# A decoder layer on one core: VectorE takes the products of the sample tokens' attention, and its loads go to GpSimd's queue

## The chip, the core and the metric

The kernel runs on one core of one Trainium2 chip. The metric is the device time of one execution in microseconds. The kernel before takes 1683.91 us, the median of three runs (1677.45 to 1688.59). A profiled execution of it took 1681.99 us, of which the profile's span, from the first to the last instruction, is 1680.2 us.

## What is computed

One layer of a hybrid decoder, for 1024 prompt tokens and 32 sample tokens (8 sequences of 4 tokens, with caches). From the normalised input a projection gives a convolution branch, queries, keys and values of 12 heads, and two gates. The heads stand in three groups of four with window and dilation (128, 1), (512, 4), (2048, 16). What matters here is the attention of the sample tokens, whose keys and values come mostly from the caches:

```python
def _dilated_sample(q, k_all, v_all, slopes, window, dil, L):
    ...
    j = jnp.arange(window // dil + 1)
    idx = L + jnp.arange(T)[:, None] - j[None, :] * dil
    kg = k_all[:, jnp.maximum(idx, 0)]
    vg = v_all[:, jnp.maximum(idx, 0)]
    s = jnp.einsum('bthd,btjhd->bhtj', q, kg) * (1.0 / math.sqrt(Dh))
    s = jnp.where(idx >= 0, s - slopes * j * dil, NEG_INF)
    p = softmax(s)
    o = jnp.einsum('bhtj,btjhd->bthd', p, vg)
```

The outputs of the three groups are combined by their softmax denominators, projected, gated, mixed with the convolution branch and added to the input; a SwiGLU feed-forward layer, a gated per-layer embedding and a final norm follow. (The lines above are cut and shortened.)

## The kernel before

All products of the prompt and of the projections run on TensorE. The float32 operands are split into a high and a low part, and each product takes three matmuls (lines 120 to 122: high by high, high by low, low by high). All 1056 tokens are handled in three chunks of 352 columns. Weights come in slabs of 512 KB (`wst`, issued from SP's queue, line 93); ScalarE makes the high part (`whi`, line 103) and VectorE the low part (`wlo`, line 104).

The stages in order: the norm of the input and the embedding's projection; the projections for the convolution and the gates, with the depthwise convolution on VectorE; then, from about 336 us, the attention; the convolution's output projection (VectorE multiplies each result by its gate, `et`, line 891, 24 times, 8 tiles by 3 chunks; the gates come from `gcd`, line 886); the attention's output projection (line 956 on VectorE, line 957 on GpSimd); and then the output projection, the feed-forward layer and the tail.

The attention runs over two pairs of heads, and in each over the three groups. For each group q, k and v are projected, TensorE makes the scores of the prompt (`ps_s`, line 824, into two banks), and VectorE empties these banks with bias and row maximum (`S` and `mcol`, line 829). After the third group the prompt's softmax follows: transposes on TensorE (line 747), copies out of PSUM on ScalarE or, for pair 0, every second one on VectorE (`pt`, line 753), and the product with the values (`N`, line 724).

The attention of the sample tokens runs beside all this, without TensorE. `sample_ops(pair, g)` makes it for one pair and group. The 128 partitions hold 64 rows (32 tokens by 2 heads) twice, the halves taking 64 cached positions each. `load` fetches the bias (`sbias`, line 552) and the queries (`sq`, line 555), the latter from a scratch tensor in DRAM (`scr`, line 862) that is written after the group's projections. `steps` then goes over the 64 positions in eight tiles of 8 positions by 64 elements (`kt`, a ring of four buffers, two loads of 64 partitions each, line 584), and `new` adds a ninth tile with the new tokens' keys or values (lines 592, 595, 598). For keys, `k_part` multiplies a tile by the query on GpSimd (line 558) and sums over the elements on VectorE (line 559). `smax` makes the softmax (lines 563 to 566). For values, `v_part` multiplies by the weights on GpSimd (line 571 for the first tile, line 573 for the others) and adds up on VectorE (line 574); line 606 sums the rest. After the third group `sample_out` joins the groups (lines 610 to 636) into the 32 sample columns of `ohi` and `olo`, which the attention's output projection reads.

These steps wait in a list and are handed out between the projections, some at a time. The order in which each engine runs its instructions is then fixed before the program starts, by a scheduler that places each instruction by its priority and by its own estimates of durations. On the chip each engine's queue runs in that order, and an instruction that waits holds up all that stand behind it on the same queue. SP's queue issues nearly all loads and stores, ScalarE's the copies of the caches, GpSimd's none.

Of the kernel before, what the change touches and what calls it, by code (L numbers as in the profile page):

```python
# [13 lines left out]
OP = mybir.AluOpType  # L14
# [18 lines left out]
SOFF = (0, 132, 261, 390)  # L33
# [14 lines left out]
def hybrid_layer(ctx: ExitStack, tc: tile.TileContext, I, O):  # L48
    nc = tc.nc
    te, ve, ac, gp, sy = nc.tensor, nc.vector, nc.scalar, nc.gpsimd, nc.sync  # L50
# [253 lines left out]
    scr = [[dram.tile([3, 32, 128], F32, name=f"scr{i}{g}") for g in range(3)] for i in range(2)]  # L304
# [224 lines left out]
    CK, HK = 8, 64  # L529
    oacc = sp.tile([128, 3, 64], F32, name="oacc")  # L530
    sv = sp.tile([128, 8, 3], F32, name="sv")
    vacc = sp.tile([128, CK, 64], F32, name="vacc")
# [3 lines left out]
    def rows(t, width, first, pair, n):  # L536

        return bass.AP(tensor=t.tensor, offset=t.offset + 2 * pair * width + first,
                       ap=[[4 * width, 32], [width, 2], [1, n]])

    def sample_ops(pair, g):
        n_new = 4 if g == 0 else 1
        nk = HK + n_new
        st = {}

        def load():
            st["s"] = sp.tile([128, HK + 4], F32, name="sc", tag="sc", bufs=2)
            st["b"] = b = sp.tile([128, HK + 4], F32, name="sbias", tag="sbias", bufs=2)
            gp.memset(b[0:64, HK:], NEG)
            for hf in range(2):  # L550
                n = nk if hf else HK
                sy.dma_start(b[64 * hf:64 * hf + 64, :n], rows(I["sbias"], SOFF[3], SOFF[g] + HK * hf, pair, n))
            st["q"] = a = sp.tile([128, 64], F32, name="sq", tag="sq", bufs=2)
            for hf in range(2):
                sy.dma_start(a[64 * hf:64 * hf + 64], scr[pair][g][0].rearrange("t (e d) -> (t e) d", d=64))

        def k_part(kt, off, n):
            gp.tensor_tensor(kt, kt, st["q"][:, None, :].to_broadcast([128, n, 64]), op=OP.mult)  # L558
            ve.tensor_reduce(st["s"][:, off:off + n], kt, axis=AX, op=OP.add)

        def smax():
            s = st["s"][:, :nk]
            ve.tensor_tensor(s, s, st["b"][:, :nk], op=OP.add)
            ve.tensor_reduce(sv[:, 0, g:g + 1], s, axis=AX, op=OP.max)
            ve.tensor_scalar(sv[:, 1, g:g + 1], sv[:, 0, g:g + 1], -1.0, None, op0=OP.mult)
            ac.activation(s, s, AF.Exp, bias=sv[:, 1, g:g + 1], accum_out=sv[:, 2, g:g + 1])

        def v_part(vt, off, n):
            p = st["s"][:, off:off + n, None].to_broadcast([128, n, 64])
            if off == 0:  # L570
                gp.tensor_tensor(vacc, vt, p, op=OP.mult)
            else:
                gp.tensor_tensor(vt, vt, p, op=OP.mult)
                ve.tensor_tensor(vacc[:, :n], vacc[:, :n], vt, op=OP.add)

        def kt_tile():
            return sp.tile([128, CK, 64], F32, name="kt", tag="kt", bufs=4)

        def steps(nm, part):
            for i in range(0, HK, CK):  # L580
                def f(i=i):
                    kt = kt_tile()
                    for hf in range(2):
                        sy.dma_start(kt[64 * hf:64 * hf + 64].rearrange("p n d -> p (n d)"),
                                     rows(I[f"{nm}g{g}"], 128 * 64, (HK * hf + i) * 64, pair, CK * 64))
                    part(kt, i, CK)
                bg.append(f)

            def new():
                kt = kt_tile()  # L590
                src = scr[pair][g]["qkv".index(nm)]
                gp.memset(kt[0:64, :n_new], 0.0)
                if g == 0:
                    for j in range(4):
                        sy.dma_start(kt[64 + 16 * j:80 + 16 * j, :4],
                                     src.rearrange("(n b) (e d) -> (b e) n d", n=4, d=64))
                else:
                    sy.dma_start(kt[64:, 0], src.rearrange("t (e d) -> (t e) d", d=64))
                part(kt[:, :n_new], HK, n_new)
            bg.append(new)  # L600

        bg.append(load)
        steps("k", k_part)
        bg.append(smax)
        steps("v", v_part)
        bg.append(lambda: ve.tensor_reduce(oacc[:, g], vacc.rearrange("p n d -> p d n"), axis=AX, op=OP.add))

# [190 lines left out]
    for pair in range(2):  # L798
        S, VT = [], []
        mcol = ap_.tile([128, 3, 8, 2], F32, name="mcol", tag="mcol", bufs=2)  # L800
        for g in range(3):
# [4 lines left out]
            for i, nm in enumerate("qkv"):  # L806
                t = ap_.tile([128, T], F32, name=nm, tag=nm, bufs=1)
# [3 lines left out]
                if i == 1:  # L811

                    q, k = qkv
# [31 lines left out]
            vt = ap_.tile([128, 8, 2, 65], F32, name=f"vt{g}", tag=f"vt{g}", bufs=1)  # L845
# [14 lines left out]
            st = ap_.tile([32, 3, 128], F32, name="stok", tag="bcot", bufs=2)  # L860
# [475 lines left out]
```

## Time and profile before

| what | value |
|---|---|
| median of three runs | 1683.91 us |
| the profiled execution | 1681.99 us |
| its span | 1680.2 us |
| TensorE's mean granted clock, of full speed | 0.988 |
| VectorE busy in the span | 1038.5 us, 62% |
| GpSimd busy in the span | 200.0 us, 12% |
| SP's and ScalarE's DMA queues moved | 174.15 MB and 57.91 MB |

In the profile the engines are PE (TensorE's matmuls), PEld (its weight loads), DVE (VectorE), ACT (ScalarE), POOL (GpSimd) and SP; a q behind a name means the engine's queue, which issues DMAs. A group's row gives line, engine, operation, output <- inputs, shape and count, then busy time and mean ns of one, then the idle time of the engine just before and what ended it. A row of a timeline gives start, duration, engine and instruction, and in brackets how long the engine stood idle before and what released it. A row of the waits gives who waited for whom, us in total, times, and the longest. Matmuls overlap, so busy time on PE isn't PE at its peak; and the idle time of an engine that nobody waits for costs nothing.

### The profile page before, as it was taken

The numbers are of one execution on the slowest core, as the hardware profiler recorded it, in microseconds if no ns is written. First come the engines' busy times: TensorE is split into PE (matmuls) and PEld (weight loads), VectorE is DVE, ScalarE is ACT, GpSimd is POOL, SyncE is SP. The second block draws the span as 40 slices with busy tenths as digits, with TensorE's granted clock in tenths as the row PEclk, the third lists the DMA queues.
The fourth block names the chain that finished last, engine by engine and source line by source line (L and its number), as shares of the span: only waits on it lengthen the run. The fifth ranks groups of instructions, "written<-read, shape, count | busy, mean of one in ns | idle before, by whom it ended". The sixth has DMA issues, their size and how long they took to land.

```text
span 1680.2 us, 27443 instructions
## 1 busy us (share of the span) xinstructions
PE 1619.0 (96%) x11091; PEld 1584.8 (94%) x11091; DVE 1038.5 (62%) x1791; ACT 579.1 (34%) x1064; POOL 200.0 (12%) x178
## 2 busy tenths in 40 slices
PE   8999999999989988989999999999999999999996
PEld 7999999988889888989999999999999999999996
DVE  7799996125453656475776666676665533437666
ACT  7211223422253325342344333333333321215542
POOL 3100000005550543250000000000000000000003
PEclk9999999999999999999999999999999999999998
DMA  8535554615441457584245444432223422311422
GB/s 306 182 127 177 187 176 151 204 50 158 144 125 34 138 175 221 165 277 160 102 157 200 159 155 161 152 133 77 77 77 118 142 87 85 117 48 57 128 72 108
DMA packets 85487, 233.81 MB, mean 139 GB/s; under 512 B 14576, under 2 KB 32432, under 8 KB 84272
## 3 DMA queue, kind: packets, MB, share of 16 engines
q1 hardware_dynamic: 76272, 174.15, 32.0%
q10 hardware_dynamic: 9088, 57.91, 10.1%
q8 instruction: 87, 1.43, 0.3%
q14 instruction: 40, 0.33, 0.1%
HBM read 187.49 MB, written 88.37 MB: 164 GB/s over the span
## 4 chain that ended last, share of the span: by engine, by line
PE 40%; issue 9%; DVE 7%; DMA 4%; ACT 1%; POOL 0%; SPq 0%; DVEq 0%; ACTq 0%; POOLq 0%
PE mm L203 6%; PE mm L205 6%; PE mm L120 6%; PE mm L204 6%; PE mm L122 6%; PE mm L121 6%; DMA wst<-in_w_fu 2%; DVE wq L145 1%; PE N L724 1%; DVE hlo L209 1%; DVE ws L150 1%; DMA et<-gcd 1%; DVE hq L209 0%; DVE fg L1071 0%; DVE ga L956 0%
## 5 line engine op out<-in xcount | busy, mean ns | idle before, releaser
L120 PE MATMUL mm<-hhi,whi 128*128 128x352 f32 x1424 | 466.7, 328 | 8.4 <-ACT hhi L367 4.4
L121 PE MATMUL mm<-hlo,whi 128*128 128x352 f32 x1424 | 462.7, 325 | 2.0 <-DVE hlo L209 2.0
L122 PE MATMUL mm<-hhi,wlo 128*128 128x352 f32 x1424 | 463.4, 326 | 0.0
L203 PE MATMUL mm<-hq,wq 128*128 128x264 f32 x1232 | 350.7, 285 | 2.3 <-DVE fg L1076 1.9
L204 PE MATMUL mm<-hq,wq 128*128 128x264 f32 x1232 | 350.5, 285 | 2.0 <-DVE hq L209 2.0
L205 PE MATMUL mm<-hq,wq 128*128 128x264 f32 x1232 | 350.3, 285 | 0.0
L120 PEld LDWEIGHTS mm<-hhi,whi 128*128 128x128 f32 x1424 | 269.4, 189 | 14.6 <-ACT hhi L367 4.9
L121 PEld LDWEIGHTS mm<-hlo,whi 128*128 128x128 f32 x1424 | 270.6, 190 | 4.4 <-DVE hlo L209 2.8
L122 PEld LDWEIGHTS mm<-hhi,wlo 128*128 128x128 f32 x1424 | 270.7, 190 | 2.2 <-issue 2.0
L203 PEld LDWEIGHTS mm<-hq,wq 128*128 128x128 f32 x1232 | 232.4, 189 | 3.3 <-ACT fg L1072 2.0
L204 PEld LDWEIGHTS mm<-hq,wq 128*128 128x128 f32 x1232 | 232.6, 189 | 2.4 <-DVE hq L209 2.4
L205 PEld LDWEIGHTS mm<-hq,wq 128*128 128x128 f32 x1232 | 232.1, 189 | 0.0
L103 ACT ACTIVATE whi<-wst 128x1024 fp32r<-128x1024 f32 (+2 forms) x100 | 97.3, 974 | 316.7 <-PE mm L121 303.7
L121 PE MATMUL mm<-mid,whi 128*128 128x352 f32 x528 | 169.5, 323 | 1.6 <-DVE mid L209 1.6
L122 PE MATMUL mm<-mid,wlo 128*128 128x352 f32 x528 | 168.4, 323 | 0.0
L120 PE MATMUL mm<-mid,whi 128*128 128x352 f32 x528 | 167.6, 324 | 0.0
L104 DVE TENSOR_TENSOR wlo<-wst,whi 128x1024 fp32r<-128x1024 f32 (+2 forms) x100 | 115.6, 1157 | 63.5 <-ACT whi L103 62.2
L425 DVE SCALAR_TENSOR_TENSOR acc<-U,vec,acc 128x1024 f32<-128x1024 f32 x120 | 147.1, 1279 | 0.4
L558 POOL TENSOR_TENSOR kt<-kt,sq 128x512 f32<-128x512 f32 (+2 forms) x54 | 68.9, 1300 | 461.4 <-DMA sq<-scr 445.9
L1138 POOL TENSOR_TENSOR y<-x,r 128x704 f32<-128x704 f32 x8 | 15.2, 1944 | 883.4 <-ACT r L938 883.4
L1122 DVE TENSOR_TENSOR x<-mm,x 128x352 f32<-128x352 f32 x96 | 49.4, 523 | 106.5 <-PE mm L122 106.1
L121 PEld LDWEIGHTS mm<-mid,whi 128*128 128x128 f32 x528 | 99.1, 188 | 1.9 <-DVE mid L209 1.9
(214 smaller groups left out, 2129.7 us busy)
## 6 DMA issues: line engine op xcount, KB each, us to landing
o_rest<-in_rest ACTq DMA_DIRECT2D x32, 768.0 KB, 5.3
wst<-in_w_in SPq DMA_DIRECT2D x42, 512.0 KB, 5.3
kt<-in_kg SPq DMA_DIRECT2D x96, 128.0 KB, 2.9
kt<-in_vg SPq DMA_DIRECT2D x96, 128.0 KB, 3.2
midd<-fg ACTq DMA_DIRECT2D x44, 264.0 KB, 3.3
mst<-midd SPq DMA_DIRECT2D x22, 528.0 KB, 4.6
wst<-in_w_fg SPq DMA_DIRECT2D x22, 512.0 KB, 3.9
wst<-in_w_fu SPq DMA_DIRECT2D x22, 512.0 KB, 5.7
```

The lines of the kernel that those rows point to most:

```text
L103: last_act[0] = ac.activation(hi[:, :n, :], st[:, :n, :], AF.Copy)
L104: ve.tensor_tensor(lo[:, :n, :], st[:, :n, :], hi[:, :n, :].bitcast(F32), op=OP.subtract)
L120: te.matmul(ps, hi[:, k, :], rh, start=(i == 0), stop=False)
L121: te.matmul(ps, hi[:, k, :], rl, start=False, stop=False)
L122: te.matmul(ps, lo[:, k, :], rh, start=False, stop=(i == n - 1))
L145: ve.tensor_tensor(t[:, 1], x, t[:, 0].bitcast(F32), op=OP.subtract)
L203: te.matmul(ps, w[:, 0, i], h[:, 0, i], start=start and i == 0, stop=False, skip_group_check=True)
L204: te.matmul(ps, w[:, 0, i], h[:, 1, i], start=False, stop=False, skip_group_check=True)
L205: te.matmul(ps, w[:, 1, i], h[:, 0, i], start=False, stop=i == k - 1, skip_group_check=True)
L425: ve.scalar_tensor_tensor(acc[:, ct, :TP], U[:, ct, j:j + TP], vcol(w0 + j), acc[:, ct, :TP], op0=OP.mult, op1=OP.add)
L558: gp.tensor_tensor(kt, kt, st["q"][:, None, :].to_broadcast([128, n, 64]), op=OP.mult)
L1122: ve.tensor_tensor(x1[:, m, cs_(c)], ps[:, :C], x1[:, m, cs_(c)], op=OP.add)
```

## The change

The products of lines 558, 571 and 573 go from GpSimd to VectorE. The loads of lines 552, 555, 584, 595 and 598 go from SP's queue to GpSimd's. The memsets of lines 549 and 592 stay on GpSimd.

```diff
             for hf in range(2):
                 n = nk if hf else HK
-                sy.dma_start(b[64 * hf:64 * hf + 64, :n], rows(I["sbias"], SOFF[3], SOFF[g] + HK * hf, pair, n))
+                gp.dma_start(b[64 * hf:64 * hf + 64, :n], rows(I["sbias"], SOFF[3], SOFF[g] + HK * hf, pair, n))
...
-                sy.dma_start(a[64 * hf:64 * hf + 64], scr[pair][g][0].rearrange("t (e d) -> (t e) d", d=64))
+                gp.dma_start(a[64 * hf:64 * hf + 64], scr[pair][g][0].rearrange("t (e d) -> (t e) d", d=64))
 
         def k_part(kt, off, n):
-            gp.tensor_tensor(kt, kt, st["q"][:, None, :].to_broadcast([128, n, 64]), op=OP.mult)
+            ve.tensor_tensor(kt, kt, st["q"][:, None, :].to_broadcast([128, n, 64]), op=OP.mult)
             ve.tensor_reduce(st["s"][:, off:off + n], kt, axis=AX, op=OP.add)
...
             if off == 0:
-                gp.tensor_tensor(vacc, vt, p, op=OP.mult)
+                ve.tensor_tensor(vacc, vt, p, op=OP.mult)
             else:
-                gp.tensor_tensor(vt, vt, p, op=OP.mult)
+                ve.tensor_tensor(vt, vt, p, op=OP.mult)
                 ve.tensor_tensor(vacc[:, :n], vacc[:, :n], vt, op=OP.add)
...
                     for hf in range(2):
-                        sy.dma_start(kt[64 * hf:64 * hf + 64].rearrange("p n d -> p (n d)"),
+                        gp.dma_start(kt[64 * hf:64 * hf + 64].rearrange("p n d -> p (n d)"),
                                      rows(I[f"{nm}g{g}"], 128 * 64, (HK * hf + i) * 64, pair, CK * 64))
...
                     for j in range(4):
-                        sy.dma_start(kt[64 + 16 * j:80 + 16 * j, :4],
+                        gp.dma_start(kt[64 + 16 * j:80 + 16 * j, :4],
                                      src.rearrange("(n b) (e d) -> (b e) n d", n=4, d=64))
                 else:
-                    sy.dma_start(kt[64:, 0], src.rearrange("t (e d) -> (t e) d", d=64))
+                    gp.dma_start(kt[64:, 0], src.rearrange("t (e d) -> (t e) d", d=64))
```

The scheduler orders all engines anew from the first group's scores on. Three places:

GpSimd's queue at the last group of pair 1 (`scr_127` and `scr_128` are the scratch tensors of its second and third group), before:

```order
L558 TENSOR_TENSOR kt<-kt,sq 128x512 x6
L592 MEMSET kt 64x64
L558 TENSOR_TENSOR kt<-kt,sq 128x512 x2
L558 TENSOR_TENSOR kt<-kt,sq 128x64
L571 TENSOR_TENSOR vacc<-kt,sc 128x512
L573 TENSOR_TENSOR kt<-kt,sc 128x512 x4
L592 MEMSET kt 64x64
L573 TENSOR_TENSOR kt<-kt,sc 128x512 x3
L573 TENSOR_TENSOR kt<-kt,sc 128x64
L957 TENSOR_TENSOR ga<-ga 128x352 x24
```

and now:

```order
L584 DMA kt<-in_vg 64x1x512 x8
L555 DMA sq<-scr_128 64x64 x2
L584 DMA kt<-in_vg 64x1x512 x8
L592 MEMSET kt 64x64
L598 DMA kt<-scr_127 64x64
L584 DMA kt<-in_kg 64x1x512 x16
L592 MEMSET kt 64x64
L598 DMA kt<-scr_128 64x64
L584 DMA kt<-in_vg 64x1x512 x16
L592 MEMSET kt 64x64
L598 DMA kt<-scr_128 64x64
L957 TENSOR_TENSOR ga<-ga 128x352 x24
```

The products are gone, and loads stand in their place; the wait for the third group's queries now stands ahead of the second half of the second group's values, and 45 loads stand from that wait on.

VectorE's queue at the end of that group, in the convolution's output projection (line 891), before:

```order
L574 TENSOR_TENSOR vacc<-vacc,kt 128x512 x3
L891 TENSOR_TENSOR et<-mm,et 128x352
L574 TENSOR_TENSOR vacc<-vacc,kt 128x512
L891 TENSOR_TENSOR et<-mm,et 128x352
L574 TENSOR_TENSOR vacc<-vacc,kt 128x512 x2
L574 TENSOR_TENSOR vacc<-vacc,kt 128x64
L606 TENSOR_REDUCE oacc<-vacc 128x64
L891 TENSOR_TENSOR et<-mm,et 128x352 x3
```

and now:

```order
L891 TENSOR_TENSOR et<-mm,et 128x352
L573 TENSOR_TENSOR kt<-kt,sc 128x512
L574 TENSOR_TENSOR vacc<-vacc,kt 128x512
L891 TENSOR_TENSOR et<-mm,et 128x352
L780 RECIPROCAL rl<-misc 128x8
L573 TENSOR_TENSOR kt<-kt,sc 128x512 x2
L574 TENSOR_TENSOR vacc<-vacc,kt 128x512
L573 TENSOR_TENSOR kt<-kt,sc 128x64
L891 TENSOR_TENSOR et<-mm,et 128x352
L574 TENSOR_TENSOR vacc<-vacc,kt 128x512
L574 TENSOR_TENSOR vacc<-vacc,kt 128x64
L606 TENSOR_REDUCE oacc<-vacc 128x64
```

The products stand between the evictions of line 891, of which 21 of 24 now come before the last reduce (line 606), where 15 did before.

SP's queue around the first gate loads of the convolution's output projection (line 886), before:

```order
L584 DMA kt<-in_kg 64x1x512 x7
L892 DMA gad_83<-et 128x1056
L584 DMA kt<-in_kg 64x1x512
L598 DMA kt<-scr_128 64x64
L886 DMA et<-gcd_76 128x1056
L584 DMA kt<-in_vg 64x1x512 x4
L886 DMA et<-gcd_77 128x1056
```

and now:

```order
L892 DMA gad_82<-et 128x1056
L886 DMA et<-gcd_76 128x1056
L892 DMA gad_83<-et 128x1056
L93 DMA wst<-in_w_att 128x1024
L886 DMA et<-gcd_77 128x1056
```

The cache loads that stood ahead of each gate load are gone from this queue.

## The prediction

> **What bounds the kernel now.** I read the page first, then busy time by stretches, then who waited for whom on TensorE and VectorE, then the single instructions around the longest waits.
>
> ```profile
> span 1680.2 us, 27443 instructions
> ...
> PE 1619.0 (96%) x11091; PEld 1584.8 (94%) x11091; DVE 1038.5 (62%) x1791; ACT 579.1 (34%) x1064; POOL 200.0 (12%) x178
> ...
> DVE  7799996125453656475776666676665533437666
> ...
> POOL 3100000005550543250000000000000000000003
> ```
>
> TensorE is busy 96% of the span, so a gain can only come out of its gaps. The touched work stands where POOL shows its digits in the middle, about 376 to 727 us. There VectorE is far from full. The stretch, and four pieces of it with a lower granted clock (columns: stretch, length, busy us of each engine with its instructions, granted clock, DMA share, GB/s):
>
> ```profile
> core 0: us, PE busy (x) PEld busy (x) DVE busy (x) ACT busy (x) POOL busy (x), PEclk, DMA share, GB/s
> 376.00:727.00 351.00, 325.94 (x2207) 302.23 (x2205) 185.11 (x403) 126.52 (x267) 135.88 (x124) 0.98 0.49 147
> ...
> 450.00:460.00 10.00, 7.86 (x38) 6.71 (x36) 8.18 (x24) 1.71 (x3) 7.18 (x7) 0.83 0.49 131
> 490.00:500.00 10.00, 5.93 (x34) 5.21 (x33) 5.58 (x8) 10.00 (x30) 8.44 (x9) 0.83 0.46 138
> 590.00:600.00 10.00, 9.85 (x53) 9.41 (x54) 4.33 (x14) 3.22 (x7) 0.01 (x1) 0.83 0.65 181
> 630.00:640.00 10.00, 9.58 (x50) 8.47 (x51) 9.86 (x22) 4.88 (x8) 4.04 (x5) 0.83 0.64 193
> ```
>
> TensorE's idle time here is 351.0 - 325.9 = 25.1 us, and the four pieces at 0.83 cost 4 x 1.7 = 6.8 us more. Who it waited for in this stage (us in total, times, longest), and for whom VectorE waited:
>
> ```profile
> PE ps_s L824 <- DVE mcol L829: 13.0, 12, 2.4
> PE N L724 <- DVE pt L753: 3.5, 1, 3.5
> PE mm L120 <- DVE et L891: 3.4, 2, 2.1
> ...
> PE ps_s L747 <- DVE pt L753: 1.3, 1, 1.3
> ```
>
> ```profile
> DVE sc L559 <- POOL kt L558: 60.8, 34, 12.1
> DVE vacc L574 <- POOL kt L573: 31.9, 18, 3.8
> ```
>
> So TensorE lost 13.0 + 3.5 + 1.3 = 17.8 us to score and transpose banks that VectorE had not yet emptied (L829, L753), and VectorE itself stood 92.7 us behind GpSimd's products. One such place, VectorE's rows and then TensorE's:
>
> ```profile
> 451.09 0.69 DVE L574 TENSOR_TENSOR vacc<-vacc,kt 128x512 f32<-128x512 f32 x1 [3.28 <-POOL kt L573]
> 451.70 0.29 DVE L829 CUSTOM_DVE_ANT_0 S<-ps_s,bias 128x128 f32<-128x128 f32 x1
> ```
>
> ```profile
> 452.26 0.71 PE L824 MATMUL ps_s<-k,q 64*128 64x128 f32 x4 [1.09 <-DVE mcol L829]
> ```
>
> VectorE waits 3.28 us for a product, the score eviction queued behind it comes late, and TensorE stands 1.09 us. That is what the change works on.
>
> **The change, part by part.** The costs come from these groups (count, busy us, mean ns):
>
> ```profile
> L558 POOL TENSOR_TENSOR kt<-kt,sq 128x512 f32<-128x512 f32 x48 | 65.1, 1376 | 461.0 <-DMA sq<-scr 445.9 <-DMA kt<-in_kg 13.3 <-DVE sc L559 1.6
> L573 POOL TENSOR_TENSOR kt<-kt,sc 128x512 f32<-128x512 f32 x42 | 52.9, 1275 | 21.6 <-DMA kt<-in_vg 20.8 <-POOL kt L573 0.3
> L558 POOL TENSOR_TENSOR kt<-kt,sq 128x64 f32<-128x64 f32 x4 | 2.1, 528 | 0.0
> ```
>
> ```profile
> L574 DVE TENSOR_TENSOR vacc<-vacc,kt 128x512 f32<-128x512 f32 x42 | 41.8, 995 | 32.9 <-POOL kt L573 31.9
> L150 DVE TENSOR_TENSOR ws<-wst 128x512 f32<-128x512 f32 x44 | 30.2, 687 | 43.5 <-DMA wst<-in_w_fu 43.3
> L574 DVE TENSOR_TENSOR vacc<-vacc,kt 128x64 f32<-128x64 f32 x4 | 0.9, 223 | 0.2
> ```
>
> *VectorE's load.* 48 + 42 + 6 = 96 full products move to it. A 128x512 product of two SBUF tiles takes 687 ns there where GpSimd is idle (L150), so 66 us, and about 3 us for the 12 short ones (eight at 0.22 as in the last row, four between): +69 us. The same shape took 995 ns where GpSimd multiplied beside it (L574), so 42 x 0.308 = 13 us come back. Net +56 us on 185 of 351 us: 69% busy. The cover is the 92.7 us for which it stood waiting; if the loads come late instead, that cover is gone and the same score evictions queue behind a load instead of a product.
>
> *GpSimd's queue.* It loses all its products of this stage and gets every load: per head group 2 bias rows, 2 queries, 32 cache pieces, and 8 new pieces in group 0 or 2 in groups 1 and 2, so 44, 38, 38 for each of two pairs, 240 in all. From SP such an issue takes
>
> ```profile
> L584 SPq DMA_DIRECT2D kt<-in_kg x96: 528/582/1059, 53.5 to 658.6; - x96
> ```
>
> No row shows a load issued from GpSimd. Lower bound: SP's 0.58 us. Upper: GpSimd needs 528 ns for a 128x64 product where VectorE needs 223, 2.4 times, so 0.58 x 2.4 = 1.4 us. I take the middle, 1.0, because neither row is near: one is the same job on another engine, the other another job on the same engine. Two loads a tile then make 2.0 us a tile, slower than GpSimd's product of 1.3 to 1.4 us; but four tiles lie in stock (the ring has four), so a burst of nine tiles is faster in its first half and slower in its second. Does a whole group fit? The products of the six groups began at:
>
> ```profile
> 376.33 5.05 POOL L558 TENSOR_TENSOR kt<-kt,sq 128x512 f32<-128x512 f32 x4 [326.67 <-DMA sq<-scr]
> ...
> 427.34 7.29 POOL L558 TENSOR_TENSOR kt<-kt,sq 128x512 f32<-128x512 f32 x5 [19.57 <-DMA sq<-scr]
> ...
> 472.95 8.51 POOL L558 TENSOR_TENSOR kt<-kt,sq 128x512 f32<-128x512 f32 x6 [15.66 <-DMA sq<-scr]
> ...
> 555.27 4.60 POOL L558 TENSOR_TENSOR kt<-kt,sq 128x512 f32<-128x512 f32 x3 [55.12 <-DMA sq<-scr]
> ...
> 602.92 6.04 POOL L558 TENSOR_TENSOR kt<-kt,sq 128x512 f32<-128x512 f32 x4 [12.91 <-DMA sq<-scr]
> ...
> 651.04 5.02 POOL L558 TENSOR_TENSOR kt<-kt,sq 128x512 f32<-128x512 f32 x4 [15.99 <-DMA sq<-scr]
> ```
>
> The periods are 51.0, 45.6, 82.3, 47.7 and 48.1 us; at 1.0 us the groups need 44, 38, 38, 44 and 38, so each fits. The tightest is 47.7 / 44 = 1.08 us a load: above about 1.1 GpSimd's queue becomes the bound.
>
> [...]
>
> *The last group.* In the new order 45 loads stand behind the wait for the last group's queries, with half of the values of the group before still among them. Before, that wait ended at 648.27, the last reduce stood at 690.77 and the 21st of the 24 conv evictions at 703.31; the row between is the load's, with its size and its median us from issue to landing:
>
> ```profile
> 648.27 1.12 SPq L555 DMA_DIRECT2D sq<-scr  x2
> ```
>
> ```profile
> kt<-in_kg SPq DMA_DIRECT2D x96, 128.0 KB, 2.9
> ```
>
> ```profile
> 690.77 1.06 DVE L606 TENSOR_REDUCE oacc<-vacc 128x64 f32<-128x512 f32 x1
> ...
> 703.31 0.51 DVE L891 TENSOR_TENSOR et<-mm,et 128x352 f32<-128x352 f32 x1
> ```
>
> In the new order that 21st eviction (L891) follows the product of the last value tile, the 45th load after the wait. With 1.0 us a load, 2.9 us to land and two tile operations of 0.69: 648.3 + 45 + 2.9 + 1.4 = 697.6, before 703.3, so nothing on the path. Bounds: nothing at 0.58; at 1.4, 715.6, +12 us.
>
> *SP's queue* loses 240 issues. What it gains on the path is the conv gate's load, which stood behind two cache issues:
>
> ```profile
> 658.62 0.53 SPq L584 DMA_DIRECT2D kt<-in_kg  x1
> 659.24 0.76 SPq L598 DMA_DIRECT2D kt<-scr  x1
> 660.05 0.59 SPq L886 DMA_DIRECT2D et<-gcd  x1
> ```
>
> These are 1.3 us, and of the 3.4 us for L891 I take -1.4 (bounds 0 and -3.4).
>
> **Sum**, against the profiled execution's 1681.99 us (1.9 under the median of the runs, 1683.91):
> - gaps behind L829 and L753: a quarter of 17.8 goes, -4.5 (bounds -17.8 and 0, or worse if the queue binds). A quarter, since the stock of four helps only the first half of a burst, and each tile now holds VectorE for two operations of 0.69 us where it held it for one;
> - the clock that such gaps cost: a quarter of 6.8, -1.7 (bounds -6.8 and 0);
> - SP's earlier conv gate: -1.4;
> - the queries' longer way, +1 (bounds 0 and 6 x 0.6 = 3.6, one SP issue each).
>
> 1682.0 - 4.5 - 1.7 - 1.4 + 1 = 1675.4, so **1675 us**.
>
> **The rivals.**
>
> *All the gaps go* (0.18). If a load costs GpSimd no more than SP, the products never wait, and everything behind VectorE vanishes: 17.8 + 6.8 + 3.4 = 28 us, 1654. For it: 92.7 us of waiting against 56 us of new work. Against it: bursts on VectorE get longer.
>
> *No change* (0.22). The score evictions queue behind a load or a second operation as they did behind a product; gaps and clock stay, 1681, or a few more up to 1695. For it: at 451 us the wait was for one tile, and a tile every 2.0 us is no earlier. The order of the work is still fixed beforehand.
>
> *GpSimd's queue becomes the bound* (0.20, slower). From about 1.1 us a load. At 1.4 a group needs 61.6 or 53.2 us: late by 10.6 and 7.6 in pair 0, by 13.9 and 5.1 in pair 1, and 12 at the end, 49 us in all. VectorE runs in order, so evictions queue behind late tiles; I let half pass through, since TensorE has other work queued: +25, 1707. For it: 2.4 times SP's price is the only ratio a row gives. Against it: an issue moves no data through the engine. [...]
>
> **How the numbers follow.** My forecast has 0.40. The range 1657 to 1703 leaves out about one in ten on each side: the lower part of the first rival and the worst of the last. Faster by over 1% (below 1667, about what a measurement can tell here) is the first rival and a tail of the forecast, 0.22; slower by over 1% is most of the last rival and the worst of no change, 0.18; within 1%, 0.60.
>
> **What would show it.** In the changed profile: the issue of a load on POOL's queue (right if 0.9 to 1.1 us); L829 <- POOL gone from VectorE's waits and a DMA wait in its place, well under 92.7 us; TensorE's wait for L829 at 8 to 12 us instead of 13.0; L574 near 0.69 us; L606 of the last group before 703 us. A POOL queue over 1.1 us a load, with VectorE waiting for kt beyond 93 us, would make the prediction wrong, and so would a wait at L829 near zero.

## The result and the profile after

The changed kernel takes 1655.9 us (median of 4 runs, 1654.6 to 1658.9) against 1683.4 us before (4 runs, 1677.5 to 1688.6): a ratio of 0.984, 95% interval 0.981 to 0.987. The forecast was 1675 us. The time came out where the rival "all the gaps go" had put it, at 1654.

The page of the changed kernel, with the rows that answer to those of before:

```profile
span 1655.0 us, 27310 instructions
...
PE 1612.1 (97%) x11091; PEld 1578.7 (95%) x11091; DVE 1075.6 (65%) x1899; ACT 580.6 (35%) x1064; POOL 193.0 (12%) x310
...
DVE  7799996226666668585786666666665443447665
...
POOL 3300000004431444160000000000000000000003
```

VectorE has 37 us more work, and the span is 25.2 us shorter. GpSimd's digits look as they did, but they count other work: its instructions are the 178 of before, less 108 products, plus the issues of 240 loads, 310.

The stretch from 376 us to the first L956 (727 before, 703.23 now), and the only pieces of 10 us in it with a clock below 0.96:

```profile
core 0: us, PE busy (x) PEld busy (x) DVE busy (x) ACT busy (x) POOL busy (x), PEclk, DMA share, GB/s
376.00:703.23 327.23, 319.16 (x2204) 296.87 (x2203) 223.12 (x513) 126.20 (x267) 121.26 (x242) 0.99 0.52 159
470.00:480.00 10.00, 10.00 (x67) 9.77 (x67) 8.36 (x14) 3.37 (x9) 5.30 (x12) 0.88 0.37 109
480.00:490.00 10.00, 9.03 (x66) 8.54 (x66) 4.10 (x12) 10.00 (x30) 4.55 (x10) 0.95 0.35 107
620.00:630.00 10.00, 9.61 (x53) 9.36 (x54) 8.51 (x19) 0.44 (x2) 3.26 (x7) 0.83 0.75 210
```

TensorE's idle time here is 327.2 - 319.2 = 8.1 us where it was 25.1, so 17.0 us came from its gaps. The pieces with a low clock cost 1.2 + 0.5 + 1.7 = 3.4 us, an estimate, where they cost 6.8. These are 20.4 of the 24.2 us by which L956 moved (727.45 to 703.23); the other 4 us I can't assign. After L956 the two kernels run alike (952.8 and 951.8 us to the end).

Who waited for whom in this stretch, TensorE's rows first, then VectorE's (us in total, times, longest):

```profile
PE mm L120 <- DVE et L891: 2.1, 2, 1.4
PE N L724 <- DVE bcot L791: 1.3, 2, 1.0
...
PE ps_s L747 <- DVE pt L753: 0.8, 1, 0.8
...
PE ps_s L824 <- DVE mcol L829: 0.3, 1, 0.3
```

```profile
DVE S L829 <- PE ps_s L824: 15.1, 19, 2.1
...
DVE kt L558 <- DMA sq<-scr: 8.1, 1, 8.1
...
DVE kt L573 <- DMA kt<-in_vg: 6.4, 5, 2.7
...
DVE kt L558 <- DMA kt<-in_kg: 5.4, 6, 2.2
```

TensorE's 13.0 us at L829 are 0.3, and it is VectorE that now waits for TensorE there, 19 times. In place of 92.7 us behind GpSimd, VectorE waits 19.9 us for the loads of the sample attention. The prices of the moved work, from the groups, from the line of the cache loads (shortest, median and longest ns of an issue) and from the table of DMA issues (us to landing at the end of the row):

```profile
L558 DVE TENSOR_TENSOR kt<-kt,sq 128x512 f32<-128x512 f32 x48 | 32.1, 684 | 13.5 <-DMA sq<-scr 8.1 <-DMA kt<-in_kg 5.4
L574 DVE TENSOR_TENSOR vacc<-vacc,kt 128x512 f32<-128x512 f32 x42 | 28.8, 687 | 0.7
L573 DVE TENSOR_TENSOR kt<-kt,sc 128x512 f32<-128x512 f32 x42 | 28.4, 685 | 6.4 <-DMA kt<-in_vg 6.4
```

```profile
L584 POOL DMA_DIRECT2D kt<-in_kg x96: 518/538/796, 50.3 to 652.0; - x96
```

```profile
kt<-in_kg POOLq DMA_DIRECT2D x96, 128.0 KB, 2.9
...
sq<-scr POOLq DMA_DIRECT2D x12, 16.0 KB, 1.9
```

A load costs GpSimd 0.54 us, not the 1.0 that the forecast took, and lands 2.9 us after its issue, as it did from SP's queue (2.9 before).

### The profile page after: what moved, and what is told of

It reads as the page before. It is cut to its first block, busy times and chain, and to the rows that moved or that the text cites. A ratio compares the mean times of both kernels' runs of the same rounds, so it can differ in the third digit from the quotient of the medians.

```text
span 1655.0 us, 27310 instructions
## 1 busy us (share of the span) xinstructions
PE 1612.1 (97%) x11091; PEld 1578.7 (95%) x11091; DVE 1075.6 (65%) x1899; ACT 580.6 (35%) x1064; POOL 193.0 (12%) x310
## 4 chain that ended last, share of the span: by engine, by line
PE 78%; issue 10%; DVE 6%; DMA 4%; ACT 1%; POOL 1%; SPq 0%; DVEq 0%; POOLq 0%; ACTq 0%
PE mm L120 16%; PE mm L122 16%; PE mm L121 16%; PE mm L205 8%; PE mm L203 8%; PE mm L204 8%; PE ps_s L824 2%; PE N L724 1%; DMA et<-gcd 1%; DMA kt<-in_vg 1%; DVE hlo L209 1%; PE ps_s L747 1%; DVE hq L209 0%; DVE vacc L574 0%; DMA wst<-in_w_fg 0%
## 5 line engine op out<-in xcount | busy, mean ns | idle before, releaser
L104 DVE TENSOR_TENSOR wlo<-wst,whi 128x1024 fp32r<-128x1024 f32 (+2 forms) x100 | 112.6, 1127 | 86.2 <-ACT whi L103 84.9
L1138 POOL TENSOR_TENSOR y<-x,r 128x704 f32<-128x704 f32 x8 | 15.2, 1946 | 883.0 <-ACT r L938 883.0
L121 PEld LDWEIGHTS mm<-mid,whi 128*128 128x128 f32 x528 | 99.1, 188 | 1.9 <-DVE mid L209 1.9
L120 PEld LDWEIGHTS mm<-mid,whi 128*128 128x128 f32 x528 | 98.6, 188 | 1.9 <-ACT mid L208 1.9
```

Source lines behind the costliest of these rows:

```text
L104: ve.tensor_tensor(lo[:, :n, :], st[:, :n, :], hi[:, :n, :].bitcast(F32), op=OP.subtract)
L120: te.matmul(ps, hi[:, k, :], rh, start=(i == 0), stop=False)
L121: te.matmul(ps, hi[:, k, :], rl, start=False, stop=False)
```

## The experiments

Two theories stood at the start. **W**: TensorE's gaps were VectorE's waiting behind GpSimd's products, so moving the products alone brings the gain. **Q**: the loads come earlier from a queue of their own. **C** is a third: GpSimd's products slowed VectorE's. e1 to e4 take the change apart. Each ratio is against the kernel before, run beside it on the same chip, with its 95% interval.

### One half at a time: e1 and e2

e1, products only (L571 and L573 likewise; all loads left on `sy`):

```diff
         def k_part(kt, off, n):
-            gp.tensor_tensor(kt, kt, st["q"][:, None, :].to_broadcast([128, n, 64]), op=OP.mult)
+            ve.tensor_tensor(kt, kt, st["q"][:, None, :].to_broadcast([128, n, 64]), op=OP.mult)
```

> Only the products go to VectorE; all loads stay on SP's queue. Theory W (waiting: the gain came because VectorE no longer stands behind GpSimd's products of 1.3 to 1.4 us, so the score evictions are on time): nearly the whole gain without the moved loads, 1655 to 1664 us, TensorE's wait for L829 under 3 us (13.0 before, 0.3 in the changed kernel). Theory Q (queue: the loads leave SP's queue, where they stood among weights and stores, and come early): most of the gain missing, 1672 to 1683 us, and 30 us or more of VectorE's waits for kt on a DMA in place of the 92.7 us on GpSimd.

Measured: 1685.1 us, ratio 1.002 (1.000 to 1.003). **No gain**; W falls. VectorE's waits and TensorE's:

```profile
DVE kt L558 <- DMA sq<-scr: 24.9, 4, 7.7
...
DVE kt L573 <- DMA kt<-in_vg: 16.2, 19, 4.4
...
DVE kt L558 <- DMA kt<-in_kg: 10.6, 10, 1.8
```

```profile
PE mm L120 <- DVE et L891: 8.0, 3, 3.6
PE ps_s L824 <- DVE mcol L829: 4.4, 3, 2.7
```

VectorE waits 51.7 us for loads, as Q foresaw, though the time is above Q's range too. TensorE's wait at L829 is a third of what it was, but 8.0 us stand at L891 where 3.4 stood, and over the 384 us from 376 the granted clock is 0.96 (0.98 before, 0.99 in the changed kernel): what was won at one place was lost at others. One late load, VectorE's rows and then TensorE's:

```profile
448.25 0.69 DVE L573 TENSOR_TENSOR kt<-kt,sc 128x512 f32<-128x512 f32 x1 [4.37 <-DMA kt<-in_vg]
...
451.62 0.69 DVE L573 TENSOR_TENSOR kt<-kt,sc 128x512 f32<-128x512 f32 x1
452.23 0.29 DVE L829 CUSTOM_DVE_ANT_0 S<-ps_s,bias 128x128 f32<-128x128 f32 x1
```

```profile
452.79 1.43 PE L824 MATMUL ps_s<-k,q 64*128 64x128 f32 x7 [2.66 <-DVE mcol L829]
```

After a wait of 4.37 us, six tile operations in a row stand ahead of the score evictions in VectorE's queue, and TensorE waits 2.66 us for the first of these.

e2, loads only: the diff of the change without its three lines of products.

> Only the loads go to GpSimd's queue; the products stay on GpSimd. Theory W: no gain, since VectorE still stands behind the products; rather a loss, since a tile now takes GpSimd 1.38 us of product and 2 x 0.54 us of issues, 2.5 us: 1683 to 1700 us, VectorE's wait for GpSimd at 90 us or more, TensorE's wait for L829 at 13 us or more. Theory Q: 1657 to 1672 us, with the waits of VectorE on GpSimd cut at least by half.

Measured: 1700.1 us, ratio 1.012 (1.009 to 1.015), slower. Neither half gains, and both together gain 27 us: the prices of the parts don't add. The time is at the end of W's range, but not for W's reason: VectorE waits 30 us for GpSimd where W had 90 or more, as Q foresaw, and the time isn't Q's. TensorE's waits:

```profile
PE misc L619 <- DVE kt L618: 17.9, 1, 17.9
...
PE misc L612 <- DVE sv L610: 5.8, 1, 5.8
```

and the last sums of the six groups (L606; first and last start), in e2 and in the changed kernel:

```profile
L606 DVE TENSOR_REDUCE oacc<-vacc x6: 1011/1076/1084, 442.6 to 757.2; 128x64 f32<-128x512 f32 x6
```

```profile
L606 DVE TENSOR_REDUCE oacc<-vacc x6: 1045/1066/1094, 416.5 to 680.9; 128x64 f32<-128x512 f32 x6
```

In e2 TensorE's matmuls never wait at L829, but the sample attention ends 76 us later than in the changed kernel, and TensorE waits for its end (L612, L619).

### A dearer load, and a shadow: e4 and e3

e4, every cache load cut into two of 32 partitions (`src` as before, `part_src` its r-th half):

```diff
-                        gp.dma_start(kt[64 * hf:64 * hf + 64].rearrange("p n d -> p (n d)"),
-                                     rows(I[f"{nm}g{g}"], 128 * 64, (HK * hf + i) * 64, pair, CK * 64))
+                        for r in range(2):
...
+                            gp.dma_start(dst[32 * r:32 * (r + 1)], part_src)
```

> The changed kernel with each cache load cut into two of 32 partitions, so 432 issues in GpSimd's queue where there were 240. If the prediction's threshold holds (above about 1.1 us a load the queue is the bound; 2 x 0.54 = 1.08 us is just below) the time stays within 6 us of the changed kernel's 1656, with VectorE's waits for kt on DMA up from 20 us to 30 to 50. If a load's way through GpSimd's queue decides already (theory Q), TensorE's wait for L829 comes back to 5 to 13 us, 1663 to 1680 us. If the price of an issue goes by its partitions or bytes and not by the DMA, 0.27 us each, nothing changes at all.

Measured: 1728.6 us, ratio 1.028 (1.025 to 1.031), far over all three expectations. An issue of 32 partitions takes 0.52 us, where one of 64 took 0.54 in the changed kernel, so at these two sizes the price goes by the DMA and not by its size, and a load costs 1.04. But VectorE's waits for loads stay small (11.2, 8.2 and 3.1 us); the last sum comes at 785.5, and TensorE loses its time at the end (lines 616, 623 and 960 here are 612, 619 and 956 elsewhere):

```profile
PE misc L616 <- DVE sv L614: 23.6, 1, 23.6
PE misc L623 <- DVE kt L622: 13.2, 2, 11.7
PE mm L120 <- DVE ga L960: 13.1, 7, 7.4
```

If the loads don't hold VectorE, why is the sample attention so late? Because in VectorE's queue it stands late. That pointed to the order.

e3, as e1, and a product on GpSimd that nobody needs beside each full tile:

```diff
+            if n == CK:
+                gp.tensor_tensor(dum, idle[:, None, :].to_broadcast([128, n, 64]), st["s"][:, off:off + n, None].to_broadcast([128, n, 64]), op=OP.mult)
```

> As the products-only kernel, and GpSimd multiplies a scratch tile of the same shape (128x512) after each of the 96 full tiles, for which nobody waits (its result is left unused; the ring of cache tiles has three buffers instead of four to make room). Theory C (contention: the gain came because GpSimd's products slowed VectorE's work beside them, 995 instead of 687 ns at L574): at least 10 us above the products-only kernel, near 1670 to 1680 us. Theory W: VectorE's two-tile operations go up from 0.69 towards 1.0 us, up to 0.3 x 200 = 60 us more of VectorE's time in the worst case, but with the cover of its idle time: within 6 us of the products-only kernel.

Measured: 1703.7 us, ratio 1.013 (1.010 to 1.017), 18 us above e1: by its text a point for C. But the ring of three buffers and the new instructions changed the order too, so it decides nothing; e11 repeats it with the order held.

### The order: e7, e8 and e9

Counted from the built programs: how many of L829's score evictions (48 for each pair of heads, 16 for each group) stand in VectorE's queue ahead of each group's last sum (L606). The expectations on record call them pairs of evictions; they are single ones.

| kernel | pair 0, groups 0, 1, 2 | pair 1, groups 0, 1, 2 (L891 ahead) | last L606, us |
|---|---|---|---|
| before | 24, 42, 48 | 76, 92 (0), 96 (15) | 690.8 |
| changed | 32, 48, 48 | 80, 96 (9), 96 (21) | 680.9 |
| e1 | 24, 44, 48 | 78, 96 (0), 96 (19) | 696.7 |
| e2 | 40, 48, 72 | 96 (11), 96 (24), 96 (24) | 757.2 |
| e4 | 44, 48, 80 | 96 (18), 96 (24), 96 (24) | 785.5 |

In the changed kernel the scheduler laid five of the six groups' ends later, behind evictions that before and in e1 stood after them (pair 0's third group alone stands as it did); in e2 and e4 it laid most of them later still. So a new theory, **P** (plan): the gain is that order. To test it, an order is held by edges between neighbours in one engine's list that ask only for the order of issue and wait for nothing:

```diff
+def _pin(tc, nc):
+    by = {i.name: i for i in nc.cur_bb.bb.instructions}
+    for order in _ORDER.values():
+        seq = [by[f"I-{n}"] for n in order.split()]
+        for first, then in zip(seq, seq[1:]):
+            tc.add_manual_dep(then, first.name, mybir.DependencyInfo(
+                mybir.DependencyClass.NoSync, mybir.DependencyReason.DATA), reason="order")
...
         hybrid_layer(tc, I, O)
+        _pin(tc, nc)
```

`_ORDER` holds the lists of TensorE, VectorE and ScalarE of the other kernel; the queues of SP and GpSimd are left to the scheduler. e7 is e1 in the changed kernel's order:

> Products on VectorE, all loads on SP's queue, as the products-only kernel (1685 us), but the order of the instructions on TensorE, VectorE and ScalarE is held by edges to that of the changed kernel. Theory P (plan: the scheduler, seeing the loads on another queue, laid the tile operations more thinly among the evictions, and that order is the gain): 1655 to 1664 us, VectorE's waits for kt on DMA under 30 us where the products-only kernel had 52. Theory Q (queue: loads that stand alone in a queue are issued early, loads among SP's weights and stores late): 1672 to 1690 us, those waits at 40 us or more.

Measured: 1661.6 us, ratio 0.984 (0.983 to 0.986): **the whole gain with the loads on SP's queue**. e8 is the changed kernel in e1's order:

> The mirror: products on VectorE and loads on GpSimd's queue, as the changed kernel (1656 us), but TensorE, VectorE and ScalarE held to the order of the products-only kernel. Theory P: 1676 to 1690 us, with VectorE's waits for kt on DMA near 50 us. Theory Q: 1655 to 1664 us, with those waits near 20 us. Between, say 1668, both take part.

Measured: 1686.5 us, ratio 1.000 (0.998 to 1.002): **none of the gain with the loads on GpSimd's queue**. VectorE's waits in e7 and then in e8:

```profile
DVE kt L558 <- DMA kt<-in_kg: 8.5, 7, 2.9
DVE kt L558 <- DMA sq<-scr: 7.9, 1, 7.9
...
DVE kt L573 <- DMA kt<-in_vg: 6.2, 5, 3.0
```

```profile
DVE kt L558 <- DMA sq<-scr: 29.0, 6, 8.2
DVE kt L558 <- DMA kt<-in_kg: 15.8, 14, 2.6
DVE kt L573 <- DMA kt<-in_vg: 14.9, 22, 2.1
```

The same loads are late or in time by where the tile operations stand, not by their queue: 22.6 and 59.7 us. Q falls, and with it my reading of e1's 51.7 us. e7's row at the place of e1's stall shows what the order does:

```profile
450.28 0.29 DVE L829 CUSTOM_DVE_ANT_0 S<-ps_s,bias 128x128 f32<-128x128 f32 x1 [0.65 <-PE ps_s L824]
...
454.73 0.29 DVE L829 CUSTOM_DVE_ANT_0 S<-ps_s,bias 128x128 f32<-128x128 f32 x1 [0.46 <-PE ps_s L824]
```

Three tile operations stand ahead of each of these evictions, where e1 had six, and VectorE is there before TensorE.

e9 is e4 (a load at 1.04 us) in the changed kernel's order:

> Each cache load in two pieces on GpSimd's queue (1.04 us a load, 1729 us with the scheduler's own order), with TensorE, VectorE and ScalarE held to the order of the changed kernel. Theory P: the 73 us were lost because the scheduler laid the tile operations late, not because the loads came late: 1655 to 1668 us, VectorE's waits on DMA under 50 us. Theory of the prediction (from about 1.1 us a load the queue itself is the bound): 1690 us or more, VectorE's waits on DMA at 80 us or more.

Measured: 1672.7 us, ratio 0.991 (0.989 to 0.993), between the two texts. Against the kernel before, each beside it, e4 lost 46.5 us, e9 gained 14.3 (from 1687.0) and the changed kernel 27.5. So of the 74 us between e4 and the changed kernel some 61 were the order and 13 are left for the dearer load itself, with VectorE's waits for loads at 20.8 + 19.4 + 8.1 + 5.6 = 54 us.

### The ring: e6

Both lines of `kt` with `bufs=2` in place of 4, the order left to the scheduler.

> The changed kernel with two cache tiles in the ring in place of four (its order is the scheduler's own). If a stock of tiles is what keeps VectorE fed: with two, a tile needs 1.1 us of issues, 3 us to land and 1.4 us of work for every second one, some 2.7 us a tile and 297 us for 108 tiles where 327 are there; late tiles then stop the evictions, 1675 to 1720 us, VectorE's waits on DMA over 80 us. If the stock hardly matters, because the order leaves time between the tiles: 1655 to 1665 us.

Measured: 1694.0 us, ratio 1.004 (1.002 to 1.006), and VectorE's waits for cache pieces and queries are 35.9 + 29.2 + 8.1 = 73 us. But TensorE waits only 0.2 us at L829; it loses 12.0 us at L956 and 7.5 at L619, as the last sum comes at 748.7. So the loss is a late end, and the ring's own part in it isn't told apart, since the order changed with the ring.

### Neither half, and contention: e10 and e11

e10 is the kernel **before**, products on GpSimd and loads on SP, with the changed kernel's order:

> The kernel before, products on GpSimd and loads on SP, with TensorE, VectorE and ScalarE held to the order of the changed kernel (VectorE without the 108 products). Theory P alone (the order is the whole gain, neither the products' engine nor the loads' queue matters): 1655 to 1668 us, VectorE's waits on GpSimd under 45 us where they were 92.7, TensorE's wait for L829 under 3 us. If the products on VectorE matter besides: 1672 to 1690 us, waits on GpSimd at 60 us or more, since in this order a pair of product and sum stands close together and a product takes GpSimd 1.3 us.

Measured: 1660.5 us, ratio 0.986 (0.983 to 0.990). **The order alone brings the gain.** TensorE's wait at L829, 13.0 us before, and VectorE's waits on GpSimd, 92.7 us before:

```profile
PE ps_s L824 <- DVE mcol L829: 0.3, 1, 0.3
```

```profile
DVE sc L559 <- POOL kt L558: 22.8, 15, 9.1
...
DVE vacc L574 <- POOL kt L573: 12.9, 8, 2.6
```

Work done by TensorE in the same 384 us, before, in the changed kernel and in e10:

```profile
376.00:760.00 384.00, 355.11 (x2382) 330.03 (x2381) 217.69 (x461) 140.19 (x294) 163.47 (x148) 0.98 0.52 161
```

```profile
376.00:760.00 384.00, 372.71 (x2522) 347.52 (x2521) 266.18 (x588) 145.55 (x303) 150.03 (x266) 0.99 0.55 172
```

```profile
376.00:760.00 384.00, 372.27 (x2519) 346.92 (x2518) 229.11 (x479) 146.13 (x304) 159.77 (x148) 0.99 0.55 172
```

140 matmuls more in the changed kernel, at 384 / 2522 = 0.152 us each, are 21 us, an estimate, and e10 has 137 of them.

e11 is e7 with the useless products of e3 (two of 128x128 a tile, the ring at four):

```diff
+            for j in range(0, n - n % CK, 4):
+                gp.tensor_tensor(dum, both[:, None, :].to_broadcast([128, 2, 64]), st["s"][:, off + j:off + j + 2, None].to_broadcast([128, 2, 64]), op=OP.mult)
```

> Products on VectorE, loads on SP, the order of the changed kernel (1661.6 us), and GpSimd multiplies a scratch tile of 128x128 twice beside each of the 96 full tiles, unused by anyone; the ring keeps its four buffers. Theory C (contention with GpSimd's SBUF traffic cost the time): VectorE's tile operations at 0.9 to 1.0 us instead of 0.69 wherever they overlap, and 8 us or more above the kernel without them, 1670 to 1685 us. Theory P: 1658 to 1668 us, the slowdown is covered by VectorE's idle time.

Measured: 1660.9 us, ratio 0.987 (0.983 to 0.990), as e7. VectorE's value tiles (lines 576 and 577 here are 573 and 574) are slower beside GpSimd, and it costs nothing:

```profile
L576 DVE TENSOR_TENSOR kt<-kt,sc 128x512 f32<-128x512 f32 x42 | 32.9, 791 | 3.6 <-DMA kt<-in_vg 3.6
...
L577 DVE TENSOR_TENSOR vacc<-vacc,kt 128x512 f32<-128x512 f32 x42 | 31.2, 742 | 0.7
```

These products are smaller than the kernel's own, so e11 alone would be a weak witness. e10 is the strong one: there L574 takes 1047 ns beside GpSimd's full products (995 before), and the gain is there. C falls as the cause, though its effect is measured: the value tiles take 791 and 742 ns here against 685 and 687 in the changed kernel.

### Which engine's order, and which part of it: e12 to e18

e12 and e13 move a part of the loads, on e1 and in the scheduler's own order: e12 line 584 to GpSimd, e13 lines 552, 555, 595 and 598.

```diff
-                        sy.dma_start(kt[64 * hf:64 * hf + 64].rearrange("p n d -> p (n d)"),
+                        gp.dma_start(kt[64 * hf:64 * hf + 64].rearrange("p n d -> p (n d)"),
```

> Products on VectorE; the 192 cache loads on GpSimd's queue, the bias, query and new-token loads on SP's; the scheduler's own order. By its order alone (30, 48 and 48 pairs of score evictions stand ahead of the last tile operation of the first pair's three groups, where the changed kernel has 32, 48 and 48 and the products-only kernel 24, 44 and 48) theory P gives nearly the changed kernel's time, 1655 to 1664 us. If the query loads on a free queue were what counted: 1672 us or more.

> The complement: the bias, query and new-token loads on GpSimd's queue, the 192 cache loads on SP's; the scheduler's own order. By its order (28, 44 and 48) theory P gives a time between, nearer the products-only kernel: 1666 to 1682 us. If the query loads on a free queue were what counted: 1655 to 1662 us.

Measured: 1668.5 us (0.990, 0.987 to 0.993) and 1667.0 us (0.990, 0.986 to 0.993). Both have some 60% of the gain. e13 is in its range, e12 is not: the three counts alone don't tell the time.

e14 holds VectorE's list alone on the kernel before, e15 those of TensorE and ScalarE alone; the scheduler lays out anew what isn't held.

> The kernel before, with VectorE alone held to the order of the changed kernel; TensorE and ScalarE are left to the scheduler. If VectorE's order carries the gain: 1655 to 1666 us, TensorE's wait for L829 under 3 us. If the orders of TensorE or ScalarE are needed as well: 1670 us or more.

> The kernel before, with TensorE and ScalarE held to the order of the changed kernel; VectorE is left to the scheduler, which then sets 28, 48 and 48 pairs of score evictions ahead of the last tile operation of the first pair's groups (24, 42 and 48 before, 32, 48 and 48 in the changed kernel). If VectorE's order carries the gain: a part of it, 1663 to 1676 us. If TensorE's and ScalarE's orders carry it: 1655 to 1663 us.

Measured: e14 1662.3 us (0.988, 0.987 to 0.990), most of the gain; e15 1683.2 us (1.000, 0.998 to 1.001), nothing, outside both of its ranges, though its counts (28, 48, 48) are near the changed kernel's. In e15 VectorE waits 58.2 + 14.7 = 73 us for GpSimd. TensorE's wait at L829 is down to 2.3 us, but it waits once for long at another place:

```profile
PE mm L120 <- DVE et L891: 12.0, 2, 11.4
```

So it is **VectorE's list** that carries the gain, and in more places than the ends of the groups.

e16 seeks the same lateness by one edit on the kernel before; e17 is the edit on e1, e18 on the changed kernel:

```diff
-                pump(PACE)
+                ins = next(i for i in reversed(nc.cur_bb.bb.instructions) if i.engine == mybir.EngineType.DVE)
+                with tc.issue_after(ins):
+                    pump(PACE)
```

> The kernel before and one edit to its order: at the pump after each projection, what the pumped steps put on an engine's queue of VectorE stands behind the last VectorE instruction that was traced before. That gives 32, 48 and 48 pairs ahead of the first pair's three ends, and 5 and 13 of L891 ahead of the last two (9 and 21 in the changed kernel). Theory P: the gain without the change, 1655 to 1666 us. If only the very order of the changed kernel does it: 1672 us or more.

> The same edit on the products-only kernel (1685 us): 32, 48 and 48 pairs, and 3 and 11 of L891. Theory P: 1652 to 1664 us, at or a little below the changed kernel, because the last group ends earlier. If the loads on SP's queue hold it back: 1668 us or more.

> The same edit on the changed kernel (1656 us). If the edit is of itself what held e16 and e17 back to half of the gain (they stood at TensorE's waits for the softmax's maxima, L683 and L709): 1664 to 1674 us. If what holds them back is that their tile operations leave less room at the third group's softmax, which the scheduler does otherwise when it sees the loads on GpSimd's queue: 1652 to 1660 us, and, if below 1654, a version faster than both.

Measured: e16 1672.6 us (0.994, 0.992 to 0.996), e17 1672.1 us (0.994, 0.993 to 0.996), e18 1657.6 us (0.985, 0.983 to 0.988). e16 and e17 have the changed kernel's counts for pair 0 (32, 48, 48) and wait only 0.3 us at L829, but have only four tenths of the gain. The longest waits that are left in e16 stand at the prompt's softmax and its maxima:

```profile
PE N L724 <- ACT pt L751: 5.5, 2, 4.5
PE misc L683 <- ACT stok L863: 3.5, 1, 3.5
PE misc L683 <- DVE mrow L689: 3.0, 1, 3.0
```

By its text e17 is in the range where the loads on SP's queue hold it back; e7, with its loads there and 1661.6 us, speaks against that, and e17 alone can't decide it, since the scheduler's order differs too. e18 shows that the edit isn't of itself the cost. No version beat the changed kernel clear of the noise: e18, e10, e7, e11 and e14 lie between 1657 and 1663 us.

**What stays open.** Which rows of VectorE's list matter besides those at L829 was not separated. Nor is it shown why the scheduler lays the sample tiles later when their loads stand on GpSimd's queue; the runs show only that it does. And whether the two halves of the change are worth a few us at a fixed order can't be told: 0.984 (0.981 to 0.987) with both and 0.986 (0.983 to 0.990) with neither overlap.

## Why the prediction was wrong

- **What bounds the kernel: right.** The gain came from the places named. Of the 17.8 us behind L829 and L753, 0.3 + 0.2 + 0.8 = 1.3 are left, and the clock's 6.8 us are 3.4.
- **VectorE's load: right in its prices.** A product takes 684 to 688 ns as L150 had it, and L574 fell from 995 to 687. The net is +38 us in the stretch, not +56. A part of this is overlap: in the changed kernel an L574 starts at 504.84 us and the next L573 at 505.45, 0.61 apart and each 0.69 long, and the sum of durations counted that twice. Other operations became shorter as well (L104 from 1418 to 1221 ns).
- **GpSimd's price: mis-sized**, 1.0 us where 0.54 was measured, just under the lower bound of 0.58. The nearer row was SP's issue of the same load. No run shows the term of +1 for the queries' longer way: from issue to landing a query takes 1.9 us from GpSimd's queue in the changed kernel, and took 2.0 from SP's before.
- **The queue as a bound.** No run had a load above the threshold of 1.1 us, the forecast's estimate from the groups' periods, so it stays untested. It is no sharp edge: just below it, with two issues of 0.53 a load and the order held (e9), some 13 us of the gain are lost already. What spoke against the rival in which GpSimd's queue becomes the bound, that an issue moves no data through the engine, agrees with the changed kernel: from GpSimd an issue takes 0.52 us for a query's 16 KB and 0.54 for a cache piece's 128 KB.
- **The last group: right that nothing is on the path**, and earlier than forecast, 679.5 us for the 21st L891 against 697.6. Its queries were issued at 624.4, where 648.3 stood, because everything ahead was 24 us earlier. But the loads didn't set this end, as the forecast had it: its own sum with 0.54 a load gives 624.4 + 24.3 + 2.9 + 1.4 = 653.0. The operations stand as late in VectorE's list.
- **SP's queue:** -1.4 forecast for L891, 3.4 to 2.1 measured. Whether the queue did it isn't shown, and the agreement may be luck: with the loads on SP and the same order, e7 has 5.6 there and e10 2.7.
- **"A quarter of 17.8 goes": the step that failed.** It priced tiles that come sooner or later into an order that stays: the stock of four, two operations a tile. The order was what changed, and the wait at L829 went to 0.3 us, which the prediction had named as a sign that it was wrong. The change is to the engine and the queue of 348 instructions, but the scheduler places every instruction by them, and moved four of the six groups' ends behind 4 to 8 more score evictions and two behind 6 and 9 more of L891's. I used the listing of that order for the last group only; the counts of the first pair, 24 against 32, stood in it.
- **The rival that came true did so for another reason.** "All the gaps go, if a load costs GpSimd no more than SP" met its condition (0.54) and its time (1654). Yet e10 loses the gaps with every load on SP and every product on GpSimd, and e8, with both moved, takes 1686.5 us and still waits 5.4 at L829. "No change" had argued that the order is fixed beforehand; it is, but anew for each kernel.

## What to carry to other kernels

Where a scheduler sets the order, an edit's effect on the order can be larger than the work it moves: list the orders of both programs, count what now stands ahead of each instruction that the bound engine waits for, and price that first. To learn which of the two a gain is, hold the new order on the old code and the old order on the new code; here the two runs took the place of any argument about engines and queues. And filler work in VectorE's queue had a best lateness here: too early it stood unready before work that was on time (e1: TensorE waited 2.66 us behind it at one place), too late its own end was waited for (17.9 us at L619 in e2, 23.6 at L616 in e4).

## What the runs showed of the hardware

A load issued from GpSimd costs its queue 0.54 us for 64 partitions of 2 KB (median, changed kernel) and 0.52 for 32 (e4), so at these sizes it goes by the DMA, and it is no dearer than from SP (0.58 before). Over the 384 us from 376, TensorE is idle in e1 for 27.0 us at a granted clock of 0.96, and in e7, the same products in another order, for 15.2 us at 1.00.
